# An encoder block with a hand-built instruction list: first head stacked in one step, its value product ahead, 42 idle products behind the routing, new prices in the list

## The chip, the cores and the metric

The kernel runs on one core of one Trainium2 chip. The metric is the device time of one execution in microseconds (us). Several executions of the same kernel agree within about 0.1% here, so a difference of 0.2% (2 us) is about what a measurement of this kernel can tell from no change.

The engines of the core carry these names in the profile: PE is TensorE (matrix products and transposes), PEld its loading of weights, DVE is VectorE, ACT is ScalarE, POOL is GpSimd and SP is SyncE, which only issues DMAs here. Each engine works through its own instructions in the order in which the program lists them; an instruction that waits for another engine holds up everything behind it on its own engine.

## The reference: what is computed

512 tokens and 16 learned "meta" tokens (528 rows of width 1024) go through one block: a normalisation, one wide projection, two attention branches side by side, and then a mixture of 16 experts.

```
u = rms_norm(h, g_mix);  z = u @ w_in                       # 528 x 6656
qa, ka, va, qb, kb, vb, ga, gb = split(z)
# branch a: 8 heads, each two maps of 64 channels
w  = softmax(q1 k1^T / 8 + alibi) - lam * softmax(q2 k2^T / 8 + alibi)
oa = rms_norm(w va, g_subln)
# branch b: 8 query heads on 2 key heads, 128 channels, axial rotary
qh, kh = rope(rms_norm(qb)), rope(rms_norm(kb));  ob = softmax(qh kh^T / sqrt(128)) vb
h = h + (sigmoid(ga) * (oa @ w_branch_a) + sigmoid(gb) * (ob @ w_branch_b)) @ w_out
# experts: each of 16 takes its 66 best tokens
aff = softmax(rms_norm(h) @ w_router);  top_aff, idx = top_k(aff^T, 66)
y = (silu(xs w_gate) * (xs w_up)) w_down * top_aff;  h = h + scatter_add(idx, y)
out = rms_norm(h, g_final), meta rows dropped
```

## The kernel before

**Products.** Every operand of a product is split into a high and a low half (`hi_lo`: ACT casts the high half, DVE or POOL subtracts to get the low one), and a product is three matmuls: high by high, high by low, low by high. `project(j, ...)` multiplies one block of 128 weight columns, number `j` of a fixed list, with all 528 rows in two halves of 256 and 272 rows: 8 chunks of 128 by three matmuls, 24 matmuls for each half. Its result stands in a PSUM tile `pz` (two of them) and is copied out by the function `evac`. `split_weights(j)` makes the halves `wh` and `wl` of block j (two buffers of each); the raw block `wraw` (512 KB, three buffers) is fetched on SP's queue as soon as a buffer is free.

**A heads.** For head h three blocks are projected: queries, keys, values (`proj_a`, lines 937 to 943). A head's two maps have 64 channels each, and the kernel stacks high and low halves of one map above each other on the 128 partitions so that one matmul does two of the three products. Moving 64 partitions to the other 64 is done by DMAs on SP's queue (`move`, `stack_q`, `stack_k`, lines 910 to 935): nine for each head, some of which wait for others, since they overwrite what the earlier ones read. The stacked tiles are `qh`, `kbuf`, and `kbh` or `kbl`. The scores land in `psc`, DVE adds the bias and takes the row maximum, ACT makes the exponentials (`sn`), PE turns them (`ptr <- sn`), and `apply_v` multiplies them with the values. `norm` then normalises each head's output: PE sums squares and turns them (`ptr <- rows`), DVE adds them up, POOL takes the inverse root with a power and four small steps on `cols` (`root`, line 453), and PE spreads the result (`pz <- cols`).

**B heads.** The same with one map, 128 channels and no stacking. The scale of a head's scores comes from `cols`; DVE scales the exponentials (`pb`) and PE turns them (`ptr <- pb`).

**The order.** It isn't left to a scheduler on the chip. While the program is built, a class `Pace` (line 126) keeps a time for each engine and each tile: an operation starts when its engine is free and its inputs are ready, and lasts as long as `Op.price` (line 101) says. Matmuls are put out in the order of the code; operations of ACT, DVE and POOL wait in a list and are put out when, by these times, their turn has come (`pump`). `mix` runs one head's attention as `main` and the projections of the next head as `fill`: at each step it takes whichever is ready by the clock of `Pace`. The prices so fix the order on every engine, and the chip then runs that order with its own durations.

**The first head.** Nothing can be mixed with it. `first_heads` (line 975) projects first halves of queries and keys, then their second halves, then the values; only then are the moves of `stack_q` and `stack_k` listed. The fill of the next head follows, and then the first scores.

**Routing.** After the output projection the router's scores are sorted by 27 steps on DVE, the indices `idxu` are made, and POOL gathers the rows of the first experts from DRAM (`gather`, line 1490; calls from line 1554). The first expert's products wait for the first gather. The expert loop then runs weights, 2 MB a piece, through casts and subtractions (`eh`, `el`) into PE.

Of the kernel before, what the change touches and what calls it, by code (L numbers as in the profile page):

```python
# [20 lines left out]
P = 128  # L21
D = 1024
# [47 lines left out]
def keys(ap):  # L70
# [3 lines left out]
    width = {"kbuf": L, "rowp": D, "m1": L, "h2T": L, "xin": D, "pair": L, "obf": L, "hrow": D, "junk": D, "big": D, "first": D, "raw": D,  # L74
# [11 lines left out]
class Op:  # L86
    def __init__(self, eng, op, fn, args, kw, prio):
# [11 lines left out]
        self.cost = self.price(aps)  # L99

    def price(self, aps):
# [7 lines left out]
        if self.eng == "tensor":  # L109
            n = 1  # L110
            for d in self.kw["rhs"].shape[1:]:
                n *= d
            return max(107.0, n / 2.4 + 2.5)
        if self.eng == "scalar":
            return 65.0 + n / 1.2 + (90.0 if len(self.outs) > 1 else 0.0)
        if self.eng == "gpsimd":
            return 60.0 + n * 2.27
# [8 lines left out]
class Pace:  # L126
# [5 lines left out]
    def __init__(self):  # L132
        self.t = {}
        self.ready, self.by, self.used, self.floor, self.slots = {}, {}, {}, {}, {}
        self.pending, self.busy = [], set()
        self.prio = 1
# [38 lines left out]
    def start(self, op):  # L175
# [4 lines left out]
        for a in op.names:  # L180
            lat = self.LAT if dma or self.by.get(a) != op.eng else 0.0 if op.eng == "tensor" else 130.0
            start = max(start, self.ready.get(a, 0.0) + lat)
        return start

    def emit(self, op):
# [7 lines left out]
        else:  # L193
            end = self.t[eng] = start + op.cost
        for a in op.tiles:
# [97 lines left out]
def block_kernel(ctx: ExitStack, tc: tile.TileContext, x, meta_tokens, g_mix, w_cols,  # L293
# [190 lines left out]
    def split_weights(j, upto=2):  # L484
# [3 lines left out]
        if j not in split:  # L488
            split[j] = (wk.tile([P, NC, P], F32R, tag="wh", bufs=2, name="wh"),
                        wk.tile([P, NC, P], F32R, tag="wl", bufs=2, name="wl"), [0])  # L490
# [153 lines left out]
    def load_bias(h):  # L644
        nc.sync.dma_start(biases[:, h % 2], c_bias[h].rearrange("(i p) k -> p i k", p=P))
    load_bias(0)
# [39 lines left out]
    def values(j, v, name):  # L686
# [6 lines left out]
        yield from project(j, u_h, u_l, evac)  # L693
# [281 lines left out]
    def first_heads():  # L975
        q, k, v = open_head(0)
        for hf in range(2):
            for n, (h, l), ahead in (("qa", q, 0), ("ka", k, 1)):
                yield from project(jof[n, 0], u_h, u_l, lambda _, cs, ps: hi_lo(h[:, cs], l[:, cs], ps),
                                   only=(hf,), ahead=ahead)  # L980
            if hf == 0:
                flush("rows")
                lambdas()
        Task(stack_q(0), Need([q[1]]), ["qk0"])
        Task(stack_k(0), Need([k[1]]), ["qk0"])
        yield from values(jof["va", 0], v, "v0")
# [567 lines left out]
    gather(0)  # L1554
    gather(1)
# [233 lines left out]
```

## Time and profile before

| | us |
|---|---|
| median of 3 runs | 1044.0 (1043.59 to 1044.48) |
| the profiled execution, its own time | 1043.74 |
| its span, first to last instruction | 1042.0 |
| PE busy | 958.8 (92% of the span) |
| DVE busy | 729.0 (70%) |
| ACT busy | 629.6 (60%) |
| POOL busy | 311.3 (30%) |

The profiled execution stands 0.3 us under the median, and 1.7 us of it lie outside the span. The span falls into stages: normalisation and the first head's projections up to about 43 us, A heads to 310, B heads to 580, gates and the output projection to 712, routing to 740, experts and the final normalisation to the end. PE is the engine that is nearly always busy, so times of PE's waits are the places where time can be had, if the engine that is waited for can do its part earlier or PE has other work to do first.

### The profile page before, as it was taken

The page shows a single profiled execution, that of the slowest core. Times are in us where ns is not written, and L with a number is a line of the kernel's source. Part 1 is how long each engine was busy: PE and PEld are TensorE (multiplying, and loading weights), DVE is VectorE, ACT ScalarE, POOL GpSimd, SP SyncE. Part 2 cuts the span into 40 slices and gives each one's busy share as a digit, 9 for nine tenths or more (in the row PEclk, how much of TensorE's full clock was granted, in tenths as well). Part 3 has the DMA queues.
Part 4 walks back from the last instruction along what each step waited for, and adds up shares of the span by engine and source line. Part 5 has one row for each costly group of instructions (what it writes and reads, how often), then busy time and mean ns, then how long its engine had stood idle before and what let it go on. Part 6 is the DMA issues. An engine that isn't in the chain of part 4 may idle for free.

```text
span 1042.0 us, 18075 instructions
## 1 busy us (share of the span) xinstructions
PE 958.8 (92%) x6835; PEld 830.5 (80%) x6835; DVE 729.0 (70%) x1390; ACT 629.6 (60%) x1297; POOL 311.3 (30%) x354
## 2 busy tenths in 40 slices
PE   4799999999999999999999999995699999999994
PEld 4799989999988899999999999994356666666563
DVE  6357777767774766665665336557699999999886
ACT  5366656666665545555545533344488888888784
POOL 3233232322443434423332400000324342423141
PEclk9999999999999999999999999998799999999997
DMA  7543544444122122121122464834799999999965
GB/s 253 161 136 94 144 124 121 123 108 125 57 72 72 52 72 71 52 72 52 62 62 63 139 201 165 321 121 165 237 355 372 354 374 353 371 348 364 369 218 182
DMA packets 59617, 186.43 MB, mean 179 GB/s; under 512 B 6766, under 2 KB 6907, under 8 KB 59530
## 3 DMA queue, kind: packets, MB, share of 16 engines
q0 software_dynamic: 26544, 98.37, 27.3%
q1 hardware_dynamic: 32378, 84.74, 26.2%
q10 hardware_dynamic: 608, 2.16, 0.7%
q8 instruction: 54, 0.88, 0.3%
q14 instruction: 33, 0.27, 0.1%
HBM read 164.23 MB, written 10.76 MB: 168 GB/s over the span
## 4 chain that ended last, share of the span: by engine, by line
PE 65%; DVE 15%; ACT 7%; issue 4%; POOL 4%; DMA 3%; SPq 1%; POOLq 0%; ACTq 0%; DVEq 0%
PE pz L199 40%; PE psc L199 21%; PE ptr L199 5%; DVE sn L199 3%; POOL cols L199 3%; ACT sn L199 2%; DVE cols L199 1%; DVE pb L199 1%; SPq L199 1%; DVE wtl L199 1%; DVE ls L199 1%; DVE zb L199 1%; DMA zp<-zb 1%; DMA xin<-in_x_dram 1%; POOL wl L199 1%
## 5 line engine op out<-in xcount | busy, mean ns | idle before, releaser
L199 PE MATMUL pz<-u_h,wh 128*128 128x256 f32 (+1 forms) x832 | 246.2, 296 | 5.9 <-ACT u_h L199 1.8
L199 POOL TENSOR_TENSOR wl<-wraw,wh 128x512 fp32r<-128x512 f32 x106 | 142.1, 1347 | 345.9 <-ACT wh L199 341.0
L199 PE MATMUL pz<-u_l,wh 128*128 128x256 f32 (+1 forms) x832 | 238.1, 286 | 0.5 <-DVE u_l L199 0.5
L199 PE MATMUL pz<-u_h,wl 128*128 128x256 f32 (+1 forms) x832 | 238.0, 286 | 0.6 <-DVE wl L199 0.6
L199 DVE TENSOR_TENSOR el<-raw,eh 128x1024 fp32r<-128x1024 f32 x180 | 212.8, 1224 | 8.1 <-ACT eh L199 7.2
L199 ACT CAST eh<-raw 128x1024 fp32r<-128x1024 f32 x180 | 181.3, 1049 | 20.6 <-PE pz L199 13.5
L199 PEld LDWEIGHTS pz<-u_h,wh 128*128 128x128 f32 x832 | 158.1, 190 | 9.2 <-DVE kbuf L199 2.3
L199 PEld LDWEIGHTS pz<-u_l,wh 128*128 128x128 f32 x832 | 158.3, 190 | 0.7 <-DVE u_l L199 0.7
L199 PEld LDWEIGHTS pz<-u_h,wl 128*128 128x128 f32 x832 | 158.1, 190 | 0.8 <-DVE wl L199 0.8
L199 PE MATMUL psc<-eh,xh 128*66 128x512 f32 (+1 forms) x272 | 104.8, 385 | 2.7 <-ACT hid L199 2.2
L199 ACT CAST wh<-wraw 128x512 fp32r<-128x512 f32 x152 | 90.9, 616 | 23.4 <-PE pz L199 19.5
L199 PE MATMUL psc<-el,xh 128*66 128x512 f32 (+1 forms) x272 | 103.8, 381 | 0.1
L199 PE MATMUL psc<-eh,xl 128*66 128x512 f32 (+1 forms) x272 | 103.7, 381 | 0.0
L199 DVE TENSOR_TENSOR wtl<-ptr,wth 128x512 fp32r<-128x512 f32 (+1 forms) x72 | 46.0, 638 | 59.0 <-ACT wth L199 58.7
L199 PE MATMUL pz<-eh,hhl 128*66 128x512 f32 x224 | 70.7, 396 | 0.7 <-DVE hhl L199 0.6
L199 ACT ACTIVATE sn<-sn,nm 128x528 f32<-128x528 f32 x64 | 47.1, 735 | 35.2 <-DVE nm L199 34.8
L199 POOL DMA_INDIRECT acc<-ys,idxu x15 | 27.5, 1835 | 122.0 <-ACT ys L199 97.1
L199 ACT CAST wth<-ptr 128x512 fp32r<-128x512 f32 (+1 forms) x72 | 39.0, 542 | 40.4 <-PE ptr L199 40.0
L199 PEld LDWEIGHTS psc<-eh,xh 128*66 128x66 f32 x272 | 37.4, 137 | 25.1 <-ACT hid L199 3.2
L199 PEld LDWEIGHTS psc<-el,xh 128*66 128x66 f32 x272 | 37.3, 137 | 23.4 <-DVE el L199 0.5
L199 PEld LDWEIGHTS psc<-eh,xl 128*66 128x66 f32 x272 | 37.4, 137 | 21.8 <-DVE xl L199 0.5
L199 DVE CUSTOM_DVE_ANT_0 sn<-psc,m 128x528 f32<-128x528 f32 x64 | 44.1, 695 | 5.8 <-PE psc L199 5.8
(315 smaller groups left out, 2328.3 us busy)
## 6 DMA issues: line engine op xcount, KB each, us to landing
wraw<-in_w_in_dram SPq DMA_DIRECT2D x76, 512.0 KB, 3.6
raw<-in_w_up_dram POOLq DMA_DIRECT2D x14, 2048.0 KB, 17.3
raw<-in_w_down_dram POOLq DMA_DIRECT2D x14, 2048.0 KB, 20.2
raw<-in_w_gate_dram POOLq DMA_DIRECT2D x13, 2048.0 KB, 18.7
m<-in_c_bias_dram SPq DMA_DIRECT2D x8, 1056.0 KB, 7.0
kbuf<-kbuf SPq DMA_DIRECT2D x32, 132.0 KB, 2.4
raw<-in_w_up_dram SPq DMA_DIRECT2D x2, 2048.0 KB
raw<-in_w_gate_dram SPq DMA_DIRECT2D x2, 2048.0 KB, 10.5
```

Source lines behind the costliest of these rows:

```text
L199: op.fn(*op.args, **op.kw)
```

## The change

Five edits, of which the first sets the order of nearly the whole program:

1. `price` gets other durations: a matmul takes 0.4375 ns a column and 6 ns instead of 0.417 and 2.5; ACT's operations get 75 ns (activations) or 30 ns more; POOL's get 30 ns more, and its power takes 1150 ns instead of 71. A DVE operation with two or more inputs, none of them in PSUM, now starts behind the POOL operation that runs at that time (`port`, `pool`).
2. In `first_heads` the values' first half is projected between the first and the second halves of queries and keys. `evac_q` and `evac_k` copy the lower 64 partitions from PSUM straight to a second tile with ACT (six copies), and `stack` then needs six moves, none of which waits for another.
3. The third weight block (the values') gets buffers of its own (`wboth`, in the place of a tile that is used later), so `wh` and `wl` are free for the next block; its subtraction falls to DVE.
4. The first bias tile is fetched on POOL's queue instead of SP's.
5. 42 matmuls of 32 by 256 columns, whose result nobody reads, stand on PE between the last matmul of the routing and the first expert's transposes.

```diff
--- before.py
+++ after.py
@@ -71,7 +71,7 @@
 
     kind = ap.name.split("_")[0]
     step = ap.ap[0][0]
-    width = {"kbuf": L, "rowp": D, "m1": L, "h2T": L, "xin": D, "pair": L, "obf": L, "hrow": D, "junk": D, "big": D, "first": D, "raw": D,
+    width = {"kbuf": L, "wboth": NC * P, "rowp": D, "m1": L, "h2T": L, "xin": D, "pair": L, "obf": L, "hrow": D, "junk": D, "big": D, "first": D, "raw": D,
              "hid": FF // 2, "hhl": 2 * CAP, "xg": 4 * CAP}.get(kind, step)
     rows = {"zp": 32, "kbuf": 64, "qh": 64, "ql": 64, "kbh1": 64, "kbl1": 64}.get(kind, P) if K["kr"] else P
     if width == step and rows == P:
@@ -97,6 +97,8 @@
         self.names = self.writes.union(*map(keys, aps))
         self.tiles = {a.name for a in aps + outs}
         self.cost = self.price(aps)
+        ins = [a for a in aps if not a.name.startswith(("pz", "psc", "ptr"))]
+        self.port = eng == "vector" and "dma" not in op and len(ins) >= 2 and len(ins) == len(aps)
 
     def price(self, aps):
         n = 1
@@ -110,11 +112,14 @@
             n = 1
             for d in self.kw["rhs"].shape[1:]:
                 n *= d
-            return max(107.0, n / 2.4 + 2.5)
+            return max(109.0, n * 0.4375 + 6.0)
         if self.eng == "scalar":
-            return 65.0 + n / 1.2 + (90.0 if len(self.outs) > 1 else 0.0)
+            scaled = 75.0 if self.op == "activation" else 30.0
+            return 65.0 + scaled + n / 1.2 + (90.0 if len(self.outs) > 1 else 0.0)
         if self.eng == "gpsimd":
-            return 60.0 + n * 2.27
+            if self.kw.get("op") == OP.pow:
+                return 1150.0
+            return 90.0 + n * 2.27
         if self.op in ("tensor_scalar", "tensor_copy", "memset"):
             return 60.0 + n * 0.65
         return 60.0 + max([n] + [a.free_size() for a in aps if callable(a.free_size)]) / 0.96
@@ -133,6 +138,7 @@
         self.t = {}
         self.ready, self.by, self.used, self.floor, self.slots = {}, {}, {}, {}, {}
         self.pending, self.busy = [], set()
+        self.pool = 0.0, 0.0
         self.prio = 1
 
     def now(self):
@@ -180,6 +186,8 @@
         for a in op.names:
             lat = self.LAT if dma or self.by.get(a) != op.eng else 0.0 if op.eng == "tensor" else 130.0
             start = max(start, self.ready.get(a, 0.0) + lat)
+        if op.port and self.pool[0] < start < self.pool[1]:
+            start = self.pool[1]
         return start
 
     def emit(self, op):
@@ -192,6 +200,8 @@
             end, eng = self.t["dma"] + 850.0, "dma"
         else:
             end = self.t[eng] = start + op.cost
+            if eng == "gpsimd":
+                self.pool = start, end
         for a in op.tiles:
             self.used[a] = max(self.used.get(a, 0.0), end)
         for a in op.writes:
@@ -486,8 +496,12 @@
             return
         load_weights(j)
         if j not in split:
-            split[j] = (wk.tile([P, NC, P], F32R, tag="wh", bufs=2, name="wh"),
-                        wk.tile([P, NC, P], F32R, tag="wl", bufs=2, name="wl"), [0])
+            if j == 2:
+                both = at.tile([P, 2, NC, P], F32R, tag="wtl", name="wboth")
+                split[j] = both[:, 0], both[:, 1], [0]
+            else:
+                split[j] = (wk.tile([P, NC, P], F32R, tag="wh", bufs=2, name="wh"),
+                            wk.tile([P, NC, P], F32R, tag="wl", bufs=2, name="wl"), [0])
         wh, wl, done = split[j]
         while done[0] < upto:
             b = slice(4 * done[0], 4 * done[0] + 4)
@@ -641,9 +655,9 @@
     m1 = keep.tile([P, NC, L], F32, tag="m1", name="m1")
     biases = m1.rearrange("p (a i) l -> p a i l", a=2)
 
-    def load_bias(h):
-        nc.sync.dma_start(biases[:, h % 2], c_bias[h].rearrange("(i p) k -> p i k", p=P))
-    load_bias(0)
+    def load_bias(h, eng=nc.sync):
+        eng.dma_start(biases[:, h % 2], c_bias[h].rearrange("(i p) k -> p i k", p=P))
+    load_bias(0, nc.gpsimd)
     cosT = pb.tile([P, L], F32, name="cosT")
     sinT = pb.tile([P, L], F32, name="sinT")
 
@@ -683,14 +697,19 @@
     def proj_split(j, h, l):
         yield from project(j, u_h, u_l, lambda hf, cs, ps: hi_lo(h[:, cs], l[:, cs], ps))
 
-    def values(j, v, name):
+    def values(j, v, name, parted=False):
         box = {}
 
         def evac(hf, cs, ps):
             if hf == 0:
                 box["z"] = ftile("f0", "zv", 2, n=LX)
             nc.scalar.copy(box["z"][:, cs], ps)
-        yield from project(j, u_h, u_l, evac)
+        if parted:
+            yield from project(j, u_h, u_l, evac, only=(0,), ahead=1)
+            yield "half"
+            yield from project(j, u_h, u_l, evac, only=(1,), ahead=1)
+        else:
+            yield from project(j, u_h, u_l, evac)
         z = box["z"]
         widen(z, P)
         vh, vl, vm = v
@@ -974,16 +993,41 @@
 
     def first_heads():
         q, k, v = open_head(0)
+        kb_, qb_ = kbuf[:, 0, 2, :], kbuf[:, 0, 3, :]
+
+        def evac_q(hf, cs, ps):
+            hi_lo(q[0][:, cs], q[1][:, cs], ps)
+            nc.scalar.copy(qb_[64:, cs], ps[64:])
+
+        def evac_k(hf, cs, ps):
+            hi_lo(k[0][:, cs], k[1][:, cs], ps)
+            nc.scalar.copy(kb_[64:, cs], ps[64:])
+            nc.scalar.copy(klow[0][64:, cs], k[1][64:, cs].bitcast(F32))
+
+        def stack():
+            (qa, ql), (ka, kl) = q, k
+            move(qb_[:64], ql[64:])
+            move(qa[64:], ql[:64])
+            for a, b in ((ka, kb_), (kl, klow[0])):
+                move(b[:64], b[64:])
+                move(a[64:], a[:64])
+            yield Need([qa, qb_]), ()
+            nc.gpsimd.tensor_copy(qmeta[0][:, 0, :M], qa[:, S:L])
+            nc.gpsimd.tensor_copy(qmeta[0][:, 1, M:], qb_[:, S:L])
+
+        val = values(jof["va", 0], v, "v0", True)
         for hf in range(2):
-            for n, (h, l), ahead in (("qa", q, 0), ("ka", k, 1)):
-                yield from project(jof[n, 0], u_h, u_l, lambda _, cs, ps: hi_lo(h[:, cs], l[:, cs], ps),
-                                   only=(hf,), ahead=ahead)
+            for n, evac in (("qa", evac_q), ("ka", evac_k)):
+                yield from project(jof[n, 0], u_h, u_l, evac, only=(hf,), ahead=0)
             if hf == 0:
+                for x in val:
+                    if x == "half":
+                        break
+                    yield x
                 flush("rows")
                 lambdas()
-        Task(stack_q(0), Need([q[1]]), ["qk0"])
-        Task(stack_k(0), Need([k[1]]), ["qk0"])
-        yield from values(jof["va", 0], v, "v0")
+        Task(stack(), Need([q[1], qb_[64:], kb_[64:], klow[0][64:]]), ["qk0"])
+        yield from val
 
     for _ in first_heads():
         tick()
@@ -1552,6 +1596,9 @@
                     mm(py[f][:CAP], a[:, c, :], b[:, fs], c == 0 and n == 0, c == 3 and n == 2)
 
     gather(0)
+    pt = ptr()
+    for i in range(42):
+        mm(pt[:2 * NE, :2 * NE * NC], wr[:, i % NC, :], wr.rearrange("p c e -> p (c e)"), True, True)
     gather(1)
     load_mat(7)
     nc.gpsimd.dma_start(acc, urow[:, :D])
```

On SP's queue the first head's part reads as follows before (`wraw` are weight blocks, `m1` the bias tile, the others the stacked tiles):

```order
L199 DMA wraw_117<-in_w_in_dram 128x1024
L199 DMA m1_197<-in_c_bias_dram 128x4x528
L199 DMA wraw_238<-in_w_in_dram 128x1024
L199 DMA wraw_280<-in_w_in_dram 128x1024
L199 DMA wraw_440<-in_w_in_dram 128x1024
L199 DMA kbuf_201<-qh_206 64x528
L199 DMA kbuf_201<-ql_207 64x528
L199 DMA qh_206<-ql_207 64x528
L199 DMA kbuf_201<-kbuf_201 64x528 x2
L199 DMA kbh1_204<-kbuf_201 64x528 x2
L199 DMA wraw_486<-in_w_in_dram 128x1024
L199 DMA kbuf_201<-kbuf_201 64x528 x2
```

and in the changed kernel:

```order
L209 DMA wraw_117<-in_w_in_dram 128x1024
L209 DMA wraw_236<-in_w_in_dram 128x1024
L209 DMA wraw_281<-in_w_in_dram 128x1024
L209 DMA wraw_329<-in_w_in_dram 128x1024
L209 DMA kbuf_201<-ql_207 64x528
L209 DMA qh_206<-ql_207 64x528
L209 DMA kbuf_201<-kbuf_201 64x528 x2
L209 DMA kbh1_204<-kbh1_204 64x528
L209 DMA kbuf_201<-kbuf_201 64x528
```

Three moves are gone, the bias has left this queue, and no weight block stands between the moves any more.

On PE, a middle B head around the turning of the sums of squares (`rows2`), before. The rows with `wh` are the first of runs of alternating matmuls; "..." leaves out the rest of a run and nothing else:

```order
L199 MATMUL ptr_5862<-ident_73,rows2_93 128x128 x2
L199 MATMUL ptr_5862<-ident_73,rows2_93 16x128
L199 MATMUL pz_5815<-u_h_101,wh_5633 128x272
...
L199 MATMUL pz_5876<-oah_502,wh_5746 128x256
...
L199 MATMUL psc_5919<-kbh0_202,qh_5200 128x264
...
L199 MATMUL ptr_5931<-ident_73,pb_5853 128x128 x4
```

and in the changed kernel:

```order
L209 MATMUL ptr_5839<-ident_73,rows2_93 128x128 x2
L209 MATMUL ptr_5839<-ident_73,rows2_93 16x128
L209 MATMUL pz_5830<-u_h_101,wh_5631 128x272
...
L209 MATMUL psc_5855<-kbh0_202,qh_5202 128x264
...
L209 MATMUL pz_5830<-u_h_101,wh_5631 128x272
...
L209 MATMUL pz_5885<-oah_500,wh_5766 128x256
...
L209 MATMUL ptr_5921<-ident_73,pb_5864 128x128 x4
```

Between `rows2` and the turning of `pb` there stood 6 matmuls of 272 columns, 24 of 256 and 6 of scores; now there stand 6 of 272, 6 of scores, 12 more of 272 and 24 of 256.

On POOL, the third A head's inverse root (`cols52`; `wl` is a weight block's subtraction), before:

```order
L199 TENSOR_TENSOR wl_2093<-wraw_1723,wh_2092 128x512
L199 TENSOR_TENSOR cols52_82<-cols52_82,halfs_95 128x5
L199 TENSOR_TENSOR cols52_82<-cols52_82 128x5
L199 TENSOR_TENSOR wl_2093<-wraw_1723,wh_2092 128x512
L199 TENSOR_TENSOR cols52_82<-cols52_82 128x5
L199 TENSOR_SCALAR cols52_82<-cols52_82 128x5
```

and in the changed kernel:

```order
L209 TENSOR_TENSOR wl_2045<-wraw_1724,wh_2044 128x512 x2
L209 TENSOR_TENSOR cols52_82<-cols52_82,halfs_95 128x5
L209 TENSOR_TENSOR cols52_82<-cols52_82 128x5 x2
L209 TENSOR_SCALAR cols52_82<-cols52_82 128x5
L209 TENSOR_TENSOR cols52_82<-cols52_82 128x5
```

A subtraction stood in the middle of this chain in each of the first six A heads; it now does so in three of the six.

## Rows read from the trace of the kernel before

**Rows 1.** Stretch, length; busy us (instructions): PE, PEld, DVE, ACT, POOL; PE's clock; DMA.

```profile
42.90:49.10 6.20, 0.00 (x0) 0.01 (x1) 2.51 (x3) 0.36 (x1) 1.94 (x3) 0.87 0.96 279
49.10:54.20 5.10, 5.08 (x22) 4.91 (x23) 1.86 (x5) 1.41 (x4) 0.00 (x0) 0.50 0.75 287
62.00:310.00 248.00, 237.33 (x1936) 231.38 (x1935) 181.33 (x438) 156.40 (x423) 81.66 (x98) 1.00 0.40 113
310.00:580.00 270.00, 256.33 (x2088) 250.04 (x2088) 160.72 (x344) 140.46 (x368) 102.23 (x113) 1.00 0.21 62
728.00:730.00 2.00, 0.23 (x1) 0.13 (x1) 1.93 (x8) 0.00 (x0) 0.00 (x0) 0.50 0.00 0
```

**Rows 2.** Timeline, first head's scores on PE: start us, length, instruction [idle before, releaser].

```profile
49.12 1.47 PE L199 MATMUL psc<-kbuf,qh 128*128 128x264 f32 x4 [6.25 <-DMA kbuf<-kbuf]
```

**Rows 3.** Timeline of SP's queue, first head: start us, length of the issue.

```profile
34.63 0.56 SPq L199 DMA_DIRECT2D kbuf<-qh  x1
...
39.67 0.46 SPq L199 DMA_DIRECT2D qh<-ql  x1
...
42.81 0.54 SPq L199 DMA_DIRECT2D wraw<-in_w_in_dram  x1
43.45 1.70 SPq L199 DMA_DIRECT2D kbuf<-kbuf  x2
```

**Rows 4.** Page, part 6: moves issued, KB each, median us to landing.

```profile
kbuf<-kbuf SPq DMA_DIRECT2D x32, 132.0 KB, 2.4
```

**Rows 5.** The chain that ended last, in order of time: start us, us, what.

```profile
28.11 12.10 PE pz L199 x96
...
740.68 7.25 PE psc L199 x24
748.42 8.06 PE psc L199 x35
...
1027.07 1.29 DVE hrow L199
```

**Rows 6.** Timeline, DVE and ACT during the first projections.

```profile
17.68 0.69 DVE L199 TENSOR_TENSOR wl<-wraw,wh 128x512 fp32r<-128x512 f32 x1
...
20.55 0.37 ACT L199 CAST qh<-pz 128x256 fp32r<-128x256 f32 x1 [2.38 <-PE pz L199]
```

**Rows 7.** PE's waits in the A heads, 62 to 310 us: total, times, longest.

```profile
PE pz L199 <- POOL cols L199: 5.4, 5, 1.2
```

**Rows 8.** Timeline of the second A head's normalisation, PE, DVE and POOL.

```profile
130.43 1.95 POOL L199 TENSOR_TENSOR wl<-wraw,wh 128x512 fp32r<-128x512 f32 x1 [7.11 <-ACT wh L199]
130.48 0.76 DVE L199 SCALAR_TENSOR_TENSOR sn<-sn,ls 128x528 f32<-128x528 f32 x1
130.81 0.49 PE L199 MATMUL ptr<-ident,rows 128*128 128x128 f32 x3
...
132.81 1.17 POOL L199 TENSOR_TENSOR cols<-cols,halfs 128x5 f32<-128x5 f32 x1 [0.42 <-DVE cols L199]
133.94 1.30 POOL L199 TENSOR_TENSOR wl<-wraw,wh 128x512 fp32r<-128x512 f32 x1
136.29 0.76 PE L199 MATMUL pz<-ident,cols 128*128 128x128 f32 x5 [1.15 <-POOL cols L199]
```

**Rows 9.** PE's waits in the B heads, 310 to 580 us.

```profile
PE ptr L199 <- DVE pb L199: 9.0, 8, 1.4
```

**Rows 10.** Timeline of a middle B head, PE and DVE.

```profile
408.00 0.49 PE L199 MATMUL ptr<-ident,rows 128*128 128x128 f32 x3
...
411.34 1.32 DVE L199 TENSOR_SCALAR cols<-cols 128x5 f32<-128x5 f32 x2 [1.17 <-POOL cols L199]
414.23 0.73 PE L199 MATMUL ptr<-ident,pb 128*128 128x128 f32 x5 [1.42 <-DVE pb L199]
```

**Rows 11.** Timeline, PE and DVE at the first gather.

```profile
739.04 1.11 PE L199 MATMUL ptr<-ident,xs 66*128 66x66 f32 x8 [7.58 <-DMA xs<-urow,idxu]
...
743.21 1.23 DVE L199 TENSOR_TENSOR el<-first,eh 128x1024 fp32r<-128x1024 f32 x1 [0.87 <-PE psc L199]
```

## The prediction

> **What bounds the kernel now.** I read the busy times of the stages first, then PE's waits in each, then the timeline at the longest of them. In the A heads PE works 237.3 of 248.0 us, in the B heads 256.3 of 270.0 [rows 1]: PE sets the time there, and what it stands idle, 10.7 and 13.7 us, is the most that a better order can give. Outside the heads there are two places where it stands longer at once. Before the first scores it waits 6.25 us for the last move of the stacked keys [rows 2]; the stretch behind that wait runs at a granted clock of 0.50, the lower level of 1.2 GHz, for 5.1 us [rows 1]. And before the first expert it waits 7.58 us for the gathered rows [rows 11], again at 0.50 [rows 1], and its first 24 matmuls take 7.25 us where the next 35 take 8.06 [rows 5], 0.30 against 0.23 us each. The reader is to see that in both places the wait is paid a second time, by the slow clock behind it.
>
> **The first head.** The moves begin at 34.63; one that must wait for another goes out at 39.67, a weight block of 512 KB goes ahead of the last two at 42.81, and these go out at 43.45 [rows 3] and land just before 49.12 [rows 2], 5.5 us later, where such a move takes 2.4 in the median [rows 4]. All of this is gone in the new order: six moves for nine, none behind another, no weight block between. What has to be done first is later, however: 96 matmuls run from 28.11 for 12.10 us [rows 5], and the keys' second half is now the 72nd of them instead of the 48th. So it ends at 28.11 + 72 x 0.126 = 37.2. Three ACT copies of 0.37 us [rows 6] and a weight cast that stands between them bring the last copy to about 39.0; two issues of about half a us [rows 3] and 2.4 us to land [rows 4] give 42.1 to 42.6. PE, which ran out of work at 42.9 [rows 1], has six matmuls fewer ahead of the scores (0.7 us) and arrives at 42.2. I take a wait of 0.4, so **-5.8 us**. Its bounds are 0 (the moves land as late as before) and -6.25. With no gap PE's clock has no reason to fall, and half of the 5.1 us that ran at half speed come back: **-2.5 us**, which goes with the wait.
>
> The six extra ACT copies (6 x 0.37 = 2.2 us) lie beside PE's matmuls; ACT is busy 0.36 us in the 6.2 us of the wait [rows 1], and if they weren't hidden, they would cost their 2.2. The third weight's subtraction goes from POOL to DVE, 2 x 0.69 us [rows 6], between subtractions of `u_l` for which PE waits in this part. The bounds are 0 and 1.4, and I take the middle, **+0.7 us**. The bias on POOL's queue goes out some 25 us before its first use and costs nothing; if it came late, it would be the rival below.
>
> **The A heads.** The prices change the order; how long things take is read from the trace. PE waits 5.4 us, five times, for POOL's root [rows 7]. In the second head it took 5.5 us from the turning of the sums (130.81) to the spreading (136.29), and 1.30 of them were a weight's subtraction in the middle of the root [rows 8]. In the new order it still stands there in three of six heads. Counted in the list at the pitch of [rows 5], PE had 4.1, 4.1, 5.1, 4.1, 5.1 and 4.1 us of work between the two; against 5.5 that makes waits of 6.4, near enough to the 5.4 measured. It now has 3.8, 5.6, 1.6, 5.6, 3.8 and 5.6. The first, third and fifth head have the root in one piece, 5.5 - 1.3 = 4.2, and so wait 0.4, 2.6 and 0.4; the others don't wait. That is 3.4 for 5.4, **-2.0 us**. Bounds: -10.7, all that PE idles, and +5, if the third head's case holds in the other two of its kind as well.
>
> A row speaks against this count. POOL's subtraction at 130.43 took 1.95 us, 0.65 more than the one at 133.94, while DVE ran an addition of two SBUF tiles beside it from 130.48 [rows 8]. The new list holds DVE behind POOL but never POOL behind DVE, so it can be wrong by this much wherever the root stands close. The Trainium skill, in "SBUF — State Buffer", section "SBUF: two separate sides", says that DVE and GpSimd share one pair of ports and that whichever starts first holds it for its whole instruction while the other stands still. By that rule the sum would be that of the lock rival below; the trace agrees as far as the 1.95 against 1.30 goes.
>
> **The B heads.** PE waits 9.0 us in eight places for `pb` [rows 9]. In a middle head it is 1.42 us, and what is late is a chain: sums turned at 408.00, POOL's root, DVE's `cols` at 411.34, 1.17 us of waiting, then `pb` on DVE, and PE goes on at 414.23 [rows 10]. This chain of 6.2 us had 4.8 us of PE's work beside it. The new order puts 12 more matmuls of 272 columns there, 12 x 0.126 = 1.5 us, and so 6.3: the wait is just covered. DVE still has `cols` ahead of `pb`, so the chain itself gets no shorter. As the margin is a tenth of a us, I take 1.25 in each of six middle heads, **-7.5 us**, and nothing for the other two. Bounds: 0 and -13.7.
>
> **The gather.** The 42 products start when PE has nothing else, at 739.04 - 7.58 = 731.46 [rows 11]. At the low clock one takes about 5.1/23 = 0.22 us [rows 1], all 42 then 9.3, to 740.8, which makes the first expert 1.7 late. If the clock rises after 5.1 us of work as it did behind the first head's wait [rows 1], 23 are slow, 19 take 0.12 each, and the end is 738.9, just before the rows land. Then the transposes (1.11) take half and the 24 matmuls 5.5 for 7.25 [rows 5, 11], 2.3 us in all. Not all of it stays: DVE's fourth subtraction at 743.21 waits for PE's first matmuls [rows 11] and comes only about 1 us sooner, and DVE then has the expert loop's pieces without a gap. I take **-1.0 us**, between -2.3 and +1.7. The end of the program is reordered too: on DVE and ACT a row's normalisation goes ahead of the last hidden casts. 1.29 us [rows 5] is the bound for one step; since the rows then don't stand in the way of the last output, I take nothing.
>
> **Sum.** -5.8 - 2.5 + 0.7 - 2.0 - 7.5 - 1.0 = -18.1. The profiled execution took 1043.74 us, 1.74 more than its span; that gives 1025.6, and against the median, 0.3 higher, 1026 us. A measurement can tell about 0.2%, 2 us, from no change.
>
> **Rivals.**
> - The heads gain nothing: the waits for POOL and `pb` go, and as long ones come elsewhere, since 1.5 us of margin was taken from some other pair. For it: the third A head's 1.6 us. Against it: everything that was counted above. 1026 + 9.5 = **1035**.
> - The lock: POOL's root is held by DVE, 0.65 us longer [rows 8] in eight B heads, where the margin is 0.1, and in three A heads. 8 x 0.55 + 3 x 0.65 = 6.4, so **1032**.
> - The change doesn't do what it says: bias, weight blocks and moves meet on the DMA engines, which were at 0.96 during the wait [rows 1], and the stacked keys land as late as before. The first head's 8.3 us stay: **1034**. Against it: the weight block that stood between the moves is now fetched before them.
> - On the other side: the new order spreads a root too soon after its turning, as in the third A head, in all 16 heads. Each then waits about 2.6 us, 41.6 for the 14.4 of [rows 7, 9]; with the first head's and the gather's 8.6 gained that is +18.6, **1062**. It decides from 25.1/16 = 1.6 us for each head. Against it: in five of the six A heads the count says 0.4 or less.
> - The order is better everywhere, and PE's 24.4 us of idle time in the heads go: 1044 - 8.6 - 24.4 = **1011**.
>
> **How the numbers follow.** The sum holds with 0.45, and its own range is 1019 to 1031. The heads that gain nothing get 0.25, the lock 0.12, the late moves 0.06, the waits everywhere 0.05, no waits at all 0.07. The range 1016 to 1037 holds the sum, the lock, the late moves and most of the first rival, some 0.83; it leaves out the two ends. Only the slower rival, and a mixture around 1044, aren't faster: faster 0.92, same 0.03, slower 0.05.
>
> **What will show it.** In the profile after: first scores at 42 to 43 us, with a wait under 1 us before them and a granted clock of 1.00 behind; PE's waits for `pb` in the B heads under 2 us in all, a middle head's period 1.2 us or more shorter; its waits for POOL's root at about 3.4 in the A heads, most of it in the third; the 42 products over just before the gathered rows land, and the next 24 matmuls in about 5.5 us. A wait for the moves that is still there, or a new releaser high among PE's waits between 60 and 570 us, would make the prediction wrong.

## The result, and the profile after

The changed kernel took 1030.77 us in the median of 4 runs (1027.65 to 1033.20), the kernel before 1044.24 beside it: ratio 0.987, 95% interval [0.9842, 0.9897]. The forecast was 1026, between 1016 and 1037. The profiled execution took 1030.49 us; its span is 1028.7 us, 13.3 less than before.

Some of PE's waits, in the changed kernel's first 310 us, and all of them in its B heads (total, times, longest):

```profile
PE pz L209 <- POOL cols L209: 3.5, 2, 2.9
...
PE psc L209 <- DMA kbuf<-kbuf: 1.1, 1, 1.1
...
PE ptr L209 <- DVE wtl L209: 5.8, 4, 2.4
PE pz L209 <- POOL wl L209: 1.1, 1, 1.1
PE ptr L209 <- DVE pb L209: 0.2, 1, 0.2
```

The three waits that the prediction counted are where it put them. The move of the stacked keys is waited for 1.1 us instead of 6.25 [rows 2], POOL's root 3.5 instead of 5.4 [rows 7], nearly all of it once, and `pb` 0.2 instead of 9.0 [rows 9]. A releaser that was not there has come in: `wtl`, 5.8 us, and POOL's 2.5 us of the B heads are 1.1 now. The stretches of the changed kernel (length; busy us and instructions of PE, PEld, DVE, ACT, POOL; PE's clock; DMA share and GB/s):

```profile
24.00:29.40 5.40, 4.60 (x25) 3.80 (x26) 4.09 (x9) 1.85 (x4) 0.00 (x0) 0.69 0.30 109
62.00:310.00 248.00, 238.89 (x1956) 233.55 (x1955) 163.72 (x443) 158.47 (x429) 82.42 (x102) 1.00 0.40 112
163.90:167.90 4.00, 3.99 (x35) 3.89 (x36) 3.22 (x8) 2.63 (x6) 0.79 (x1) 1.00 0.51 199
310.00:580.00 270.00, 262.61 (x2139) 257.81 (x2138) 146.39 (x351) 145.88 (x376) 107.28 (x111) 0.99 0.24 68
483.20:486.60 3.40, 3.40 (x19) 3.40 (x18) 2.04 (x8) 0.63 (x1) 2.31 (x5) 0.53 0.00 0
730.00:733.00 3.00, 3.00 (x10) 1.65 (x8) 1.53 (x2) 1.64 (x3) 0.16 (x1) 0.57 1.01 351
```

PE is idle 9.1 us in the A heads and 7.4 in the B heads, where it was 10.7 and 13.7 [rows 1]. The clock column is the other half of the story. It gives the mean of a stretch: 0.50 is the lower level of 1.2 GHz, 1.00 the upper one of 2.4, and what lies between holds both. The stretch behind the first scores is no longer slow, but an earlier one is: the clock falls inside the first row above, stands at 0.50 to 0.51 from 26 to 32 us and is back at 1.00 from 34. Then 3.4 us at 483 are slow, and again 730 to 733. PE at its landmarks in the changed kernel (timeline):

```profile
47.20 0.63 PE L209 MATMUL psc<-kbuf,qh 128*128 128x264 f32 x3 [1.08 <-DMA kbuf<-kbuf]
...
163.91 0.76 PE L209 MATMUL pz<-ident,cols 128*128 128x128 f32 x5 [2.91 <-POOL cols L209]
...
422.06 0.55 PE L209 MATMUL ptr<-ident,rows 128*128 128x128 f32 x3 [1.25 <-DVE wtl L209]
451.55 0.55 PE L209 MATMUL ptr<-ident,rows 128*128 128x128 f32 x3 [1.08 <-DVE wtl L209]
482.30 0.55 PE L209 MATMUL ptr<-ident,rows 128*128 128x128 f32 x3 [2.36 <-DVE wtl L209]
...
717.28 0.23 PE L209 MATMUL ptr<-ident,vals 32*66 32x32 f32 x1 [8.49 <-DVE vals L209]
718.83 6.66 PE L209 MATMUL ptr<-wr 128*32 128x256 f32 x42
726.75 0.69 PE L209 MATMUL ptr<-ident,xs 66*128 66x66 f32 x8 [1.25 <-DMA xs<-urow,idxu]
728.15 0.45 PE L209 MATMUL psc<-eh,xh 128*66 128x512 f32 x1 [0.72 <-ACT xh L209]
...
735.55 0.66 PE L209 MATMUL ptr<-ident,xs 66*128 66x66 f32 x8
```

The gathered rows are transposed at 726.75 instead of 739.04 [rows 11]: 12.3 of the 13.3 us are won by then. The first 24 expert matmuls take 728.15 to 735.55, 7.4 us, no less than the 7.25 of before [rows 5]. The middle B heads follow each other at 451.55 - 422.06 = 29.49 us where it was 29.96: half a microsecond, not the 1.2 that the prediction asked for. The next pair, 482.30 - 451.55 = 30.75 us apart, holds the longest wait for `wtl`.

Where `wtl` comes from is seen on DVE, ACT and SP's queue in the B head whose wait is longest (timeline):

```profile
475.76 3.68 SPq L209 DMA_DIRECT2D zp<-zb  x4
...
478.41 0.59 ACT L209 CAST wth<-ptr 128x512 fp32r<-128x512 f32 x1 [0.42 <-PE ptr L209]
...
480.94 0.71 DVE L209 TENSOR_TENSOR zb<-zb,cosT 128x528 f32<-128x528 f32 x1 [3.03 <-DMA zp<-zb]
...
481.56 0.68 DVE L209 TENSOR_TENSOR wtl<-ptr,wth 128x512 fp32r<-128x512 f32 x1
```

DVE stands 3.03 us for the last of four moves into `zp`. The product by `cosT` is ahead of `wtl` in its list, although `wth` was ready near 479.0, and PE, which needs the buffer that `wtl` reads, waits for both. In the program's list the time of SP's queue advances by 0.5 us from its own last issue, not from the start of the DMA, so the four issues, 2.4 us in the other heads and 3.7 in this one, are counted as if they went out together.

### The profile page after: what moved, and what is told of

It is laid out like the page before. It is cut to its first block, busy times and chain, and to the rows that moved or that the text cites. A ratio compares the mean times of both kernels' runs of the same rounds, so it can differ in the third digit from the quotient of the medians.

```text
span 1028.7 us, 18155 instructions
## 1 busy us (share of the span) xinstructions
PE 963.4 (94%) x6877; PEld 836.7 (81%) x6877; DVE 688.8 (67%) x1391; ACT 632.5 (61%) x1303; POOL 313.1 (30%) x354
## 4 chain that ended last, share of the span: by engine, by line
PE 72%; DVE 9%; ACT 7%; DMA 6%; issue 3%; POOL 2%; SPq 1%; POOLq 0%; ACTq 0%; DVEq 0%
PE pz L209 45%; PE psc L209 21%; PE ptr L209 5%; DVE sn L209 2%; DMA zp<-zb 2%; SPq L209 1%; ACT sn L209 1%; POOL cols L209 1%; DMA hrow<-acc 1%; DMA xin<-in_x_dram 1%; ACT wh L209 1%; DVE wtl L209 1%; POOL zp L209 1%; ACT wth L209 1%; DVE sql L209 1%
## 5 line engine op out<-in xcount | busy, mean ns | idle before, releaser
L209 PE MATMUL pz<-u_h,wh 128*128 128x256 f32 (+1 forms) x816 | 241.2, 296 | 4.2 <-ACT u_h L209 2.6
L209 PE MATMUL pz<-u_h,wl 128*128 128x256 f32 (+1 forms) x816 | 233.6, 286 | 1.1 <-POOL wl L209 1.1
L209 PE MATMUL pz<-u_l,wh 128*128 128x256 f32 (+1 forms) x816 | 233.4, 286 | 0.5 <-DVE u_l L209 0.5
L209 PEld LDWEIGHTS pz<-u_h,wh 128*128 128x128 f32 x816 | 155.0, 190 | 6.2 <-ACT u_h L209 2.8
L209 PEld LDWEIGHTS pz<-u_h,wl 128*128 128x128 f32 x816 | 155.0, 190 | 1.3 <-POOL wl L209 1.3
L209 PEld LDWEIGHTS pz<-u_l,wh 128*128 128x128 f32 x816 | 155.2, 190 | 0.7 <-DVE u_l L209 0.7
L209 POOL DMA_INDIRECT acc<-ys,idxu x15 | 23.7, 1580 | 122.5 <-ACT ys L209 92.1
L209 ACT CAST wth<-ptr 128x512 fp32r<-128x512 f32 (+1 forms) x72 | 39.0, 542 | 29.4 <-PE ptr L209 29.1
```

Source lines behind the costliest of these rows:

```text
L209: op.fn(*op.args, **op.kw)
```

## The experiments

e1, e2, e5 and e7 ran on one chip, e6, e8, e9 and e4 on a second, e10 to e13 on a third, each time with the kernel before beside them (1044.4 to 1044.7 us in the median). Both kernels scatter by more than the 0.1% of the first few runs: the kernel before by 6.2 us in 19 runs on the first of these chips, the changed kernel by 5.5 in the 4 runs above, 11.2 in the 6 of e6 and 6.9 in the 6 of e10. So 2 us between the medians of a few runs tell little here.

**The parts one by one: e1, e2, e5.** Edit 1 alone (`price`, `port`) on the kernel before:

> The kernel before with edit 1 alone: new prices and the rule on POOL's tiles, hence nearly the whole new order; first head, third weight block, bias queue as before, no idle products. Theory A (the gain is idle time of PE taken out stage by stage): the waits for pb (9.0 us) and most of those for POOL go, the new waits for wtl (5.8) come, as in the trace of the changed kernel, where PE stands idle 2.4 us less in the A heads and 5 to 6 less in the B heads: 1044.2 - 8 = 1036, between 1034 and 1038; the wait of about 6 us before the first scores is still there. Theory B (the first head's gain is eaten by a slow clock that has only moved ahead of it, so that nearly all of the 13.5 us is the order's): 1032 or less.

Edits 2 to 4 alone:

> The kernel before with edits 2 to 4 alone: the first head's order, copies and moves, the third weight block's own buffers, the bias on POOL's queue; old prices, no idle products. Theory A: the wait before the first scores is 1 to 2 us instead of 6.25, PE's early part is 0.8 us later, and the slow stretch only changes its place: -5.2 + 0.8 - 0.4, so 1039.4, between 1038.4 and 1040.5. Theory B: a slow stretch ahead of the scores costs what the wait gave: 1042.5 or more.

The changed kernel without the products:

```diff
-    pt = ptr()
-    for i in range(42):
-        mm(pt[:2 * NE, :2 * NE * NC], wr[:, i % NC, :], wr.rearrange("p c e -> p (c e)"), True, True)
```

> The changed kernel without the 42 products. Theory A: they are worth what the two traces show between the lists and the second transposes, about 1 us, so 1031.7, between 1031 and 1032.5, with PE idle 7.6 us before the gathered rows and the next 24 matmuls in about 7.2 us. Theory C (the expert loop takes back whatever the start gains, since DVE has no gap there): no difference above the changed kernel's own scatter, 1030.8 within 0.5.

Measured: e1 1042.39 us (1038.37 to 1050.60, ratio 0.9986 [0.9965, 1.0007]), e2 1041.34 (ratio 0.9966 [0.9949, 0.9982]), e5 1031.95 (1031.11 to 1033.38). Theory B fell for e1: the prices alone are worth about 2 us (3.7 at the end of the interval), not 12. Theory A missed them too, by 6 us. e2 is 2 us short of A. The two gains, 2 and 3 us, don't add up to the 12.4 of both together (e5). Three things in the traces bear on that; how much each is worth in the medians is not shown, since the profiled executions took longer than these medians, 1046.05 us in e1 and 1044.76 in e2. First, each edit shifts the list of everything behind it: with the old prices and the new first head PE waits 5.9 us for POOL in the A heads (5.4 before), and 2.9 us for `zv` and `ls` where it waited 0.5. Second, the end is longer: PE comes to the router at 727.30 us in e1 and 726.59 in e2, 2.4 and 3.1 us ahead of the kernel before, but from there to the end it is 317.0 and 316.4 us instead of 312.3, and ACT waits 5.9 and 5.3 us for weights there, before not at all; the DMA engines bring 353 and 351 GB/s behind the gathered rows instead of 360. Third, e1's clock falls three times in the heads (stretches of e1):

```profile
46.00:52.70 6.70, 4.21 (x17) 3.94 (x18) 2.29 (x6) 0.42 (x2) 0.29 (x1) 0.50 1.00 351
199.50:202.90 3.40, 3.40 (x19) 3.11 (x17) 2.81 (x8) 2.10 (x5) 1.27 (x1) 0.51 0.25 96
493.00:496.40 3.40, 3.40 (x18) 3.40 (x17) 1.80 (x5) 0.63 (x1) 1.94 (x5) 0.52 0.00 0
```

The waits at these places are those for the moves (1.42 us at 46.16, where the first matmul is already slow, and 2.33 at 49.05), one A head's for POOL (2.91 at 198.31) and one for `wtl` (2.20 at 492.34). The last two are waits that only the new order has at this length, while it makes others shorter. In e5 the 24 expert matmuls take 7.6 us; that the products are worth 1 us (theory A) or nothing (theory C) is not shown, since the changed kernel itself scatters by more.

**The wait for wtl: e7.** The landing of every transfer 300 ns later in the list, so that `cosT` goes behind `wtl` in the four heads:

```diff
-            end, eng = self.t["dma"] + 850.0, "dma"
+            end, eng = self.t["dma"] + 1150.0, "dma"
```

> The changed kernel with one price more: a transfer's landing 300 ns later in the scheduler, which puts DVE's product zb by cosT behind wtl and wm in the four middle B heads in which PE waits for wtl, and leaves the A heads as they are. Theory D (DVE stands 1.8 to 3.0 us in front of wtl for the four moves into zp, whose issues of 0.59 us each the scheduler counts as one): the waits for wtl in these heads, 5.8 us together, go, and with them the slow stretch behind the longest of them (about 1.7 us at 485): 1030.8 - 5.8 - 1.7 to 1030.8 - 5.8, so 1023.3 to 1025. Theory E (wtl is only where it shows; the queries' chain, which then ends later, is waited for instead): 1029 to 1032, with a wait for the scores or pb of about 1 us in each of these heads.

Measured 1030.65 us (1029.51 to 1031.62): no gain over the 1030.77 of the first measurement, as theory E says. PE's waits in e7's B heads:

```profile
PE ptr L209 <- DVE pb L209: 4.1, 5, 1.3
PE pz L209 <- POOL wl L209: 1.1, 1, 1.1
PE pz L209 <- POOL cols L209: 0.3, 1, 0.3
```

Theory D's mechanism is right as far as `wtl` goes, which is gone from the list with the one reordering, but 4.1 of its 5.8 us come back as `pb`, behind the chain that now ends later. The clock, which D let rise again, fell in another place of the profiled execution, at the third A head:

```profile
162.10:168.10 6.00, 6.00 (x29) 5.59 (x30) 3.31 (x8) 2.11 (x5) 1.28 (x1) 0.52 0.34 132
```

The wait ahead of it, 2.90 us, and the order around it are those of the changed kernel, whose clock stays at 1.00 there (163.90 above). PE still comes to the router at 713.72 us, 3.6 ahead of the first profile, and loses it behind: 316.1 us to the end instead of 311.4, with 6.2 us of ACT's waiting for weights instead of 2.1.

**The clock, the end, the rule on POOL: e6, e8, e9, e4.** The changed kernel again:

> The changed kernel once more, as the base of the three kernels beside it. Theory F (its scatter is the clock: each fall of the granted clock behind a wait of PE of 2 to 3 us costs 1.7 us for every 3.4 us at 0.50, and it comes in some executions only): times between 1027 and 1034 that go down as the mean granted clock of the execution goes up, about 1 us for 0.001. Theory G (the scatter is that of the transfers): no relation between the two.

With products in two waits, past the list, so that no order changes:

```diff
             ps = pz()
+            if sums is not None and turned[0] == 3 and hf == 0:
+                for _ in range(22):
+                    tc.nc.tensor.matmul(ps[:, :256], lhsT=u_h[:, 0, :P], rhs=u_h[:, 0, :256], start=True, stop=True)
...
+        if e == NE - 2:
+            pt = ptr()
+            for i in range(14):
+                tc.nc.tensor.matmul(pt[:2 * NE, :2 * NE * NC], lhsT=wr[:, i % NC, :],
```

> The changed kernel with products that nobody reads in two waits of PE: 22 of 256 columns ahead of the third A head's spreading (a wait of 2.91 us for POOL's root) and 14 ahead of the last gate's up products (2.26 us for ACT's hid); nothing else is ordered otherwise. The waits end when they ended before, so only the clock can move the time. Theory F: no slow stretch at about 165 and 985 us in any execution, 1.5 to 4 us less than the changed kernel beside it, and less scatter. Theory G: the same time within 0.7 us.

The old prices from the expert loop on:

```diff
+    Op.old = True
     for e in range(NE - 2):
```

> The changed kernel with the old prices and without the rule on POOL from the expert loop on; all up to the gather is ordered as in the changed kernel. Theory H (the new prices made the end worse: the last up products wait 2.3 to 2.8 us for ACT's hid where they waited 1.35, and the clock falls behind it): 1 to 3 us less than the changed kernel, with that wait at 1.35 again. Theory I (the row's normalisation that goes ahead of the last hidden casts pays for it): 0 to 2 us more.

The new prices without the rule on POOL:

```diff
-        if op.port and self.pool[0] < start < self.pool[1]:
-            start = self.pool[1]
```

> The changed kernel with the new prices but without the rule that holds a DVE operation with two SBUF tiles behind POOL's. Theory J (the rule is what makes the new order good: DVE is busy 310 us between 62 and 580 us where it was 342 in the kernel before, since it no longer stands in its own instructions while POOL holds the tiles): DVE's busy time goes up by 10 to 30 us there, PE waits again for pb or POOL, and the time is 3 to 6 us above the changed kernel's. Theory K (the durations alone do it): within 1.5 us of the changed kernel.

Measured on one chip: e6 1034.37 us (1028.25 to 1039.42), e8 1030.67 (1028.02 to 1031.96), e9 1030.70 (1029.41 to 1034.50), e4 1033.63 (1029.66 to 1037.64). Theory F fell as far as the scatter goes: e6's executions of 1028.25 and of 1034.87 us have the same mean clock, 0.985, and the slowest has 0.984. Theory G, the transfers, has this for it in the profiled executions: over the 254 us behind the gathered rows the DMA engines bring 360 GB/s in the kernel before, 358 in the changed kernel's first profile, 355 in e6 and 353 in e10, and from these rows to the end it takes 303.0, 302.0, 304.7 and 307.4 us. What sets the rate of an execution is not shown. What the clock does is seen in e6's profiled execution, which is the changed kernel word for word. One of its stretches, and PE at its landmarks (timeline):

```profile
24.00:29.40 5.40, 4.52 (x37) 3.88 (x36) 4.23 (x11) 2.93 (x8) 0.00 (x0) 1.00 0.39 131
```

```profile
25.63 0.66 PE L209 MATMUL ptr<-ident,xin 128*128 128x128 f32 x4 [0.74 <-DVE u_l L209]
...
42.68 0.28 PE L209 MATMUL psc<-kbuf,qh 128*128 128x264 f32 x1
44.17 0.63 PE L209 MATMUL psc<-kbuf,qh 128*128 128x264 f32 x3 [1.21 <-DMA kbuf<-kbuf]
...
712.33 0.23 PE L209 MATMUL ptr<-ident,vals 32*66 32x32 f32 x1 [8.49 <-DVE vals L209]
...
721.71 0.68 PE L209 MATMUL ptr<-ident,xs 66*128 66x66 f32 x8 [0.27 <-DMA xs<-urow,idxu]
723.11 0.44 PE L209 MATMUL psc<-eh,xh 128*66 128x512 f32 x1 [0.72 <-ACT xh L209]
728.95 0.66 PE L209 MATMUL ptr<-ident,xs 66*128 66x66 f32 x8
...
979.36 0.48 PE L209 MATMUL psc<-eh,xh 128*66 128x256 f32 x1 [2.69 <-ACT hid L209]
```

The same instructions in the same order run at 1.00 from 24 to 29 us here and at 0.69 in the first profile. From the transposes behind the 0.74 us wait to the first score it is 42.68 - 25.63 = 17.1 us here and, with 26.17 in that profile's chain and 45.84 for the same matmul, 19.7 there: 2.6 us. The 3.4 us at 0.53 behind the wait for `wtl` are another 3.4 x 0.47 = 1.6 (in e6 this wait is 1.76 us instead of 2.36, and the clock stays at 1.00). Together they make 4.2 of the 717.28 - 712.33 = 5.0 us between the two executions at the router. Of the eleven profiled executions that have the changed kernel's first head and prices, the clock falls between 24 and 27 us in four: the first one, e4, e9 and e12. The 24 expert matmuls take 5.84 us here, 5.5 in the forecast, and 7.4 where the clock fell.

e8 is 3.7 us faster than e6, its mean clocks 0.986 to 0.989 against 0.983 to 0.985, and its products turn the 2.91 us wait into 0.27. That is the size that theory F asked for, but its mechanism is not shown. The profiles of the changed kernel (the first, e6 and e10) have no slow stretch at 165 us that the products could have taken away, and e8's own has two behind 970 us, 972 to 976 and 989 to 993, where e6's has one. And e6's median is 3 us above the same kernel's on the other chips (1030.77 and 1031.76), against which e8 gains nothing that stands out of the scatter. e9 is as far below e6 with a clock of 0.982 to 0.986, and its profile shows `hid` waited for 1.35 us at 983.89 and 2.62 at 1004.72, so neither H nor I is borne out; its cause stays open. e4 speaks for K: without the rule DVE is busy 325.7 us between 62 and 580 (310.1 with it, 342.1 before), so J's first half holds, and the time doesn't follow; but e4's runs lie 8 us apart, and 2 us would not be seen. DVE's scaling of `pb` in 62 to 580 us, changed kernel and then e4 (busy us, mean ns of one, idle before):

```profile
L209 DVE TENSOR_SCALAR pb<-pb,ls 128x528 f32<-128x528 f32 (+1 forms) x40 | 26.4, 660 | 1.1
```

```profile
L202 DVE TENSOR_SCALAR pb<-pb,ls 128x528 f32<-128x528 f32 (+1 forms) x40 | 28.1, 702 | 1.2
```

In the kernel before it took 824 ns. Most of the fall of this one duration came with the prices already.

**The weights: e10, e11, e12, e13.** In e6 ACT waits 7.9 us for weights (`raw`), all behind 900 us, and from the last expert but one's rows to the last one's it takes 20.3 us, where it takes 17.4 from one to the next in the kernel before. The base on the next chip:

> The changed kernel as the base of the three beside it, on their chip: 1029 to 1035, with ACT waiting 2 to 9 us for weights behind 900 us of the profile and none before.

Two matrices not transferred:

```diff
+        if n in (16, 17):
+            raws[n] = raws[n - len(ring)]
+            return
```

> The changed kernel without the transfers of two of the 47 weight matrices (the 17th and 18th; the pieces are split from what lies in their places from eight matrices before, so that every instruction on the engines stays): 4.2 MB less, 11.7 us of transfers at 358 GB/s. Theory L (the expert loop takes 6.3 MB in each 17.4 us, 361 GB/s, the DMA engines bring 350 to 360 at a busy share of 1.03, and the lead is used up by the last two experts): ACT's waits for weights behind 900 us are gone, the last experts take 17.4 us each, the time is 2 to 4 us below the base and scatters less. Theory M (the end's waits and the scatter come from the order of ACT and DVE and from the clock): within 1 us of the base.

One transfer moved:

```diff
     send_factors()
+    load_mat(7)
...
-        eng = nc.gpsimd if n > 6 else nc.sync
+        eng = nc.gpsimd if n > 7 else nc.sync
...
     gather(1)
-    load_mat(7)
```

> The changed kernel with one transfer moved: the eighth weight matrix is issued on SP's queue behind the router's rows instead of on POOL's behind the second gather, about 8 to 10 us earlier, where the DMA engines have a share of 0.38; no other instruction moves. Theory L: up to 5.8 us more of lead at the loop's end, ACT's waits for weights shorter by that, and 1 to 3 us less than the base. Theory N (the transfer runs beside the first gather and holds it up): the gathered rows land 2 to 5 us later than 4.4 us after the 42 products' start plus the usual wait, and nothing is won or up to 3 us lost.

And three edits together:

> The changed kernel with three edits together: the landing price of e7, the 36 products of e8, the earlier transfer of e12. If the three theories behind them hold side by side: PE idles 4 us less ahead of the router than the base, no slow stretch behind the third A head, less waiting at the end: 3 to 7 us below the base. If the loop's transfers set the end whatever comes ahead of them: no better than e12.

Measured: e10 1031.76 us (1030.01 to 1036.94), e11 1031.05 (1029.94 to 1031.93), e12 1025.57 (1024.21 to 1028.46, ratio 0.9815 [0.9802, 0.9827]), e13 1022.01 (1021.31 to 1024.00, ratio 0.9791 [0.9777, 0.9805]). ACT's waits for weights in e10:

```profile
ACT eh L209 <- DMA raw<-in_w_down_dram: 5.4, 2, 3.4
ACT eh L209 <- DMA raw<-in_w_up_dram: 1.0, 1, 1.0
ACT eh L209 <- DMA raw<-in_w_gate_dram: 0.3, 1, 0.3
```

In e11, e12 and e13 there are none, and the last two of these steps take 17.4 us where e10's take 20.0 and 22.1. From the first transposes to the end it is 1030.1 - 722.69 = 307.4 us in e10, 1029.1 - 725.73 = 303.3 in e11 and 1026.7 - 725.66 = 301.0 in e12. So theory L holds for ACT's waits. For the length of the stage it is likely only, since the changed kernel's own goes from 302.0 to 307.4. The DMA engines in e10 and then e12, ahead of the gathered rows and in the loop:

```profile
711.00:722.70 11.70, 8.18 (x47) 6.52 (x47) 7.18 (x21) 1.04 (x1) 5.29 (x5) 0.61 0.22 43
722.70:977.00 254.30, 249.01 (x1193) 148.84 (x1194) 229.00 (x257) 206.07 (x254) 91.78 (x81) 1.00 1.03 353
```

```profile
714.00:725.60 11.60, 8.45 (x46) 6.66 (x46) 7.25 (x21) 1.04 (x1) 5.12 (x5) 0.58 0.74 227
725.60:980.00 254.40, 251.17 (x1220) 152.44 (x1220) 234.22 (x264) 212.48 (x263) 79.06 (x81) 1.00 1.01 351
```

An expert takes three matrices of 2,048 KB, 6.29 MB in 17.4 us, 361 GB/s; the engines bring 353 at a share of 1.03. By this estimate some 2% are missing, and over 254 us that is some 5 us, which the last two experts wait for; in the kernel before, at 360 GB/s, ACT waits for none. e12 fills 11.6 us in which the share was 0.22, and theory N doesn't show: the rows are there 5.8 us after the gather's issue, in e10 5.9. The edit also takes an issue of 1.0 us off POOL's queue, and the third gather goes out 0.9 us sooner behind the first; the two effects were not separated. The Trainium skill, in "DMA: Bandwidth & Descriptors", section "Bandwidth", gives some 358 GB/s as the limit of one core at its memory, and 425 as measured on a core whose neighbour is idle. The 351 to 360 of the loop lie at the first; what the neighbour did is not shown. Why e11 gained only 0.7 us in the median, with 4.1 won in the profiled stage, is not settled: its profiled execution lost 3.0 us ahead of the rows, where the clock fell at 161 us, and its timed ones have clocks of 0.981 to 0.985 against 0.982 to 0.989 in e12.

e13 is the best: 22.6 us below the kernel before on its chip, 3.6 below e12, so a gain ahead of the router can reach the end once the weights are early. Its clocks are 0.986 to 0.991; its profile has no slow stretch between 21 and 700 us, where e12's has two, and PE comes to the router at 711.71 us instead of 716.30. Which of the two edits that it adds to e12 brings this was not tested.

## Why the prediction was right, and what was mis-sized

- **First head, -5.8:** right, 5.2 of it. PE came to the first score at 42.68 in e6, forecast for 42.2; the moves landed just before 44.17 there, forecast for 42.1 to 42.6, and so the wait is 1.2 us, 1.1 in the first profile, instead of 0.4. The last move went out at 39.79 in e6, about as forecast, but it was 4.4 us until PE could go on, where 2.4 had been taken; the DMA engines' share was 1.00 from 42 to 44 us.
- **Its clock, -2.5:** the step that failed. "With no gap PE's clock has no reason to fall": there was no gap, and in the profiled execution the clock fell some 20 us earlier instead, behind two short waits of 1.17 and 0.74 us (1.57 and 0.25 before), and cost 2.6. In e6 it did not. The term is worth 2.5 in one execution and nothing in the next.
- **A heads, -2.0:** right. POOL is waited for 3.5 us (forecast 3.4), 2.9 of it in the third head, where the count said 2.6. All releasers together PE idles 1.6 us less. The row that was held against the count [rows 8] does not say who held whom: POOL starts at 130.43, 0.05 us ahead of DVE, and is the one that takes longer.
- **B heads, -7.5:** mis-sized by 1.2. `pb` went as counted, 9.0 to 0.2, and PE has 6.2 us of work beside the chain in a middle head (451.55 to 457.78), 6.3 in the forecast. That the chain gets no shorter was wrong: up to the end of `pb` it takes 5.5 us there where it took 6.1, because DVE does `cols` and `pb` in 0.24 and 0.50 us instead of 1.32 each. The first rival came beside it: 5.8 us for `wtl` in four heads. With POOL's 2.5, now 1.1, PE idles 6.3 us less. The slow stretch behind the longest wait takes 1.6 of that back.
- **Gather, -1.0:** 0.9 from the router to the end in this profile, but not by its own mechanism, so by luck: the products end before the rows land, as forecast, yet the clock falls again at 730. In e6 the 24 matmuls take 5.8 us, near the 5.5 that were forecast, and the end of the loop gives it back to the weights. That the transfers of the weights bind at the end is in no term of the sum.
- **The third weight block, +0.7, and the end of the program, nothing:** not tested alone. The last up products wait 2.26 us for `hid` where they waited 1.35.
- **Sum:** up to the router, where the terms make -17.1, the profiled execution of e6, the fastest of its six, is at 712.33, 17.4 us ahead of the 729.72 of before; the first profile is 12.4 ahead, and of the 4.7 that are missing there 4.2 are the clock. Of the rivals, that heads give waits back elsewhere was right in kind. The lock on POOL's root did not show: PE waits for the root nowhere in the B heads and 3.5 us in the A heads, as counted. The others didn't happen.

## What to carry over

A wait of PE has two prices: itself, and the clock that may fall behind it in some executions and not in others. A new order that makes many waits of one microsecond into few of two to three can win less than the sum of idle time says. Where a list is written from prices, a queue's issue time has to be counted: four moves that go out one after the other were taken for one. And where the transfers fill a stage to the last percent, look at what the DMA engines do ahead of it: a load moved into such a gap is the one edit here that took over 5 us off by itself.

## What the runs showed that was not expected

- The same program with the same waits has the clock at 0.69 in one execution and at 1.00 in another (24 to 29.4 us), and at 1.00 (first profile, e6) or 0.52 (e7, e11) at the same 2.9 us wait.
- Moving one 2 MB transfer by some 10 us and to another queue, with the order of all else kept, took 6.2 us off the median (4.3 us between the extremes, 6.9 in the base).
- Two gains of 2 and 3 us, measured alone, gave 12 together; each edit reorders what lies behind it, and in the profiled executions of both the way from the router to the end is 4 to 5 us longer.
